# Two of seven Strassen sums started fresh at a change of groups and added by VectorE, with the first pairs' parts and the foldings moved in the written order

## Chip, cores, metric

One core of one Trainium2 chip runs the whole program in one launch. The time is device microseconds of one execution, as a median of three runs.

## What is computed

A hybrid decoder trunk of two layers over 256 positions of width 2048, all in float32: a short gated convolution and an MLP, then multi-head latent attention and an MLP, each followed by a layer norm of the residual. The change lies in the two MLPs:

```python
def sq_relu_mlp(x, w1, w2):          # w1: 2048 x 8192, w2: 8192 x 2048
    return jnp.square(jax.nn.relu(x @ w1)) @ w2

h = layer_norm(ALPHA * h + sq_relu_mlp(h, mlp_w1[layer], mlp_w2[layer]), ...)
```

## The kernel before

**Numbers.** A float32 factor is split into a high part, rounded by ScalarE (`hi`, L139), and the rest, subtracted by VectorE (`lo`, L140). TensorE multiplies high by high, high by low and low by high. Each weight tile of 128x1024 comes by DMA into one of seven `raw` tiles and costs one ScalarE cast and one VectorE subtraction.

**Passes and slots.** The 8192 hidden columns go in eight passes `q` of eight chunks `m` of 128 columns. In pass 0 everything is done plainly. From pass 1 on the up-projection of one chunk (a *unit*: 32 matmuls into the PSUM bank `unit`) is fused with down-projection work of an earlier chunk pair. One turn of the loop over (q, m) is a *slot*. The unit leaves its bank by `whole` (L399 on ScalarE into `t`, L400 on VectorE into `fp`), which is called the evacuation; the next unit needs the bank.

**Fast products.** For passes 1 to 6 (`FAST`; in the second MLP also half of pass 7) the down projection of a pair of chunks is done with seven products in place of eight, after Strassen and Winograd: four additions on the activations (`form`, L688 to L691; the results are split into the factors `h1a`, `h1c` and so on by `finish_pair`) and four on the weights (`prepare`, L172 to L179: `raw_t`, then the tiles `11`, `T1`, `21` and the others). Each of the seven products adds to a sum of its own in a PSUM bank. They are issued in the order of `FACTORS`: 3, 1, 5, 7, 2, 6, 4. Products of a pair lag the units by five slots.

**Groups.** The seven sums cover one group of 1024 of the 2048 output columns at a time. After four pairs of a pass the other group's turn comes: the change of groups, in the slot m = 0 of the next pass. All seven sums are then stored (`put_back`, L653) to their places in SBUF, and those of the other group are loaded into the same banks (`resume`, L738), both by ScalarE with 0.6 us copies. Sums 1, 5, 7 and 6 (`OWN`) have places of their own in `sums` and begin fresh the first time; 2, 3 and 4 have theirs in the accumulator `acc`. Four of the seven moves are spread over the slot of the change, and three lie in the next slot, which is called *crowded* in the code: there the evacuation comes ahead of the products.

**Folding.** At the end the eight additions of `fold` for each group combine the sums into `acc` (L661). The first MLP then goes on with pass 7 plainly (`down`); its residual, parked in DRAM meanwhile, comes back into the tile that `sums` had (L880, on POOL's queue; L452 is its first use). The second MLP ends with `down_late`, where the last additions (`fold_last`, L672) and the last layer norm are done on what is still in PSUM.

**Order.** Within the slots the order of the instructions of TensorE, VectorE and ScalarE is the written one: `Order.keep` ties each instruction to the one before it on its engine. Outside the slots, and on the queues of SP and POOL, a planner orders them by its own costs. `move(n)` does n of the waiting moves, `to_step(n)` brings the next slot's weight pair to its step n, `split_due` splits factors that are due, and `far` is a pair two slots ahead in the first slots of a MLP, which have no products yet.

## Time and profile before

| | |
|---|---|
| median of three runs | 2024.12 us (2024.03 to 2024.38) |
| the profiled execution | 2027.43 us, its span 2025.6 us |
| mean granted TensorE clock | 0.997 |
| busy: TensorE | 1993.8 us (98%) |
| busy: VectorE | 1754.5 us (87%) |
| busy: ScalarE | 1298.8 us (64%) |
| fused passes of the first MLP | about 452 to 1006 us of the span |
| fused passes of the second MLP | about 1408 to 1996 us of the span |

A row of a timeline gives start, duration, engine, line and operation; in brackets the idle time of the engine just before it and who ended it. A row `a <- b` of the waits gives who waited for whom: total, times and the longest. Matmuls are pipelined: one of 512 columns is shown with 0.39 us but they follow each other faster, so busy time of TensorE counts no work, while a gap in it is a gap. A row of the windows gives busy time by engine (TensorE, its weight loads, VectorE, ScalarE, POOL), then the granted clock, the DMA share and GB/s. PE is TensorE, DVE is VectorE, ACT is ScalarE.

### The profile page before, as it was taken

The page shows a single profiled execution, that of the slowest core. Times are in us where ns is not written, and L with a number is a line of the kernel's source. Part 1 is how long each engine was busy: PE and PEld are TensorE (multiplying, and loading weights), DVE is VectorE, ACT ScalarE, POOL GpSimd, SP SyncE. Part 2 cuts the span into 40 slices and gives each one's busy share as a digit, 9 for nine tenths or more (in the row PEclk, how much of TensorE's full clock was granted, in tenths as well). Part 3 has the DMA queues.
Part 4 walks back from the last instruction along what each step waited for, and adds up shares of the span by engine and source line. Part 5 has one row for each costly group of instructions (what it writes and reads, how often), then busy time and mean ns, then how long its engine had stood idle before and what let it go on. Part 6 is the DMA issues. An engine that isn't in the chain of part 4 may idle for free.

```text
span 2025.6 us, 29534 instructions
## 1 busy us (share of the span) xinstructions
PE 1993.8 (98%) x11050; PEld 1731.1 (85%) x11050; DVE 1754.5 (87%) x2539; ACT 1298.8 (64%) x1915; POOL 5.6 (0%) x27
## 2 busy tenths in 40 slices
PE   9999999999999999999999999999999999999998
PEld 8888888988888888888879998898888888888886
DVE  8667677777999999999989988777899999999998
ACT  7444445576767767677746665557667776767763
POOL 0000000000000000000000000000000000000000
PEclk9999999999999999999999999999999999999999
DMA  9766666574665566655765544565456656566554
GB/s 346 207 189 187 189 193 189 180 226 126 207 207 191 186 206 206 202 188 194 241 205 180 180 130 144 178 196 158 140 195 206 205 188 202 194 208 196 186 191 156
DMA packets 107710, 389.98 MB, mean 193 GB/s; under 512 B 11952, under 2 KB 12720, under 8 KB 107056
## 3 DMA queue, kind: packets, MB, share of 16 engines
q1 hardware_dynamic: 106560, 383.79, 59.1%
q0 software_dynamic: 864, 4.19, 0.6%
q8 instruction: 86, 1.41, 0.3%
q14 instruction: 56, 0.46, 0.1%
q10 hardware_dynamic: 144, 0.13, 0.0%
HBM read 383.87 MB, written 4.19 MB: 192 GB/s over the span
## 4 chain that ended last, share of the span: by engine, by line
PE 49%; DVE 37%; issue 7%; ACT 6%; DMA 0%; DVEq 0%; ACTq 0%
DVE lo L140 13%; PE ps_l L255 13%; PE ps_l L259 7%; DVE lo_t L140 5%; DVE raw_t L172 4%; PE ps_u L255 3%; DVE raw L179 3%; DVE raw L177 3%; DVE t L140 2%; PE ps_d L343 2%; PE ps_d L342 2%; PE ps_d L340 2%; ACT hi L139 2%; PE ps_w L289 2%; PE ps_w L288 2%
## 5 line engine op out<-in xcount | busy, mean ns | idle before, releaser
L140 DVE TENSOR_TENSOR lo<-raw,hi 128x1024 fp32r<-128x1024 f32 x710 | 853.4, 1221 | 138.9 <-ACT hi L139 69.7
L139 ACT CAST hi<-raw 128x1024 fp32r<-128x1024 f32 x710 | 729.2, 1049 | 353.7 <-DVE raw L177 141.8
L255 PE MATMUL ps_u<-xhl,hi 128*128 128x512 f32 x1792 | 624.3, 395 | 12.7 <-DVE fp L400 12.6
L259 PE MATMUL ps_u<-xhl,lo 128*128 128x256 f32 x1792 | 486.8, 281 | 0.0
L255 PEld LDWEIGHTS ps_u<-xhl,hi 128*128 128x128 f32 x1792 | 330.0, 188 | 84.7 <-DVE fp L400 18.4
L259 PEld LDWEIGHTS ps_u<-xhl,lo 128*128 128x128 f32 x1792 | 339.2, 189 | 12.3
L255 PE MATMUL ps_l<-xhl_a,hi 128*128 128x512 f32 x704 | 244.1, 393 | 0.0
L259 PE MATMUL ps_l<-xhl_a,lo 128*128 128x256 f32 x704 | 195.5, 280 | 0.0
L255 PEld LDWEIGHTS ps_l<-xhl_a,hi 128*128 128x128 f32 x704 | 132.2, 188 | 29.8
L259 PEld LDWEIGHTS ps_l<-xhl_a,lo 128*128 128x128 f32 x704 | 131.9, 188 | 0.2
L172 DVE TENSOR_TENSOR raw_t<-raw,raw 128x1024 f32<-128x1024 f32 x100 | 121.9, 1219 | 0.0
L140 DVE TENSOR_TENSOR lo_t<-raw_t,hi_t 128x1024 fp32r<-128x1024 f32 x100 | 121.9, 1219 | 0.0
L139 ACT CAST hi_t<-raw_t 128x1024 fp32r<-128x1024 f32 x100 | 105.2, 1052 | 3.9 <-DVE raw_t L172 3.9
L399 ACT COPY t<-ps_u 128x256 f32<-128x256 f32 x112 | 41.1, 367 | 89.5 <-PE ps_u L259 89.5
L255 PE MATMUL ps_l<-z,hi 128*128 128x512 f32 x240 | 82.4, 391 | 0.0
L400 DVE TENSOR_TENSOR fp<-ps_u,t 128x256 f32<-128x256 f32 x112 | 47.2, 421 | 35.3 <-ACT t L399 35.3
L289 PE MATMUL ps_w<-xd,hi 128*128 128x258 f32 x256 | 72.8, 284 | 0.0
L287 PE MATMUL ps_w<-xd,hi 128*128 128x258 f32 x256 | 72.3, 283 | 0.0
L288 PE MATMUL ps_w<-xd,lo 128*128 128x258 f32 x256 | 72.3, 283 | 0.0
L179 DVE TENSOR_TENSOR raw<-raw 128x512 f32<-128x512 f32 x100 | 69.2, 692 | 3.5
L140 DVE TENSOR_TENSOR t<-raw,t 128x512 fp32r<-128x512 f32 x100 | 68.6, 686 | 3.5 <-ACT t L139 3.5
L255 PE MATMUL ps_l<-oT,hi 128*128 128x512 f32 x208 | 71.3, 392 | 0.0
(361 smaller groups left out, 3908.2 us busy)
## 6 DMA issues: line engine op xcount, KB each, us to landing
raw<-in_w_dram SPq DMA_DIRECT2D x312, 512.0 KB, 4.2
raw<-in_w2f_dram SPq DMA_DIRECT2D x200, 512.0 KB, 4.1
raw<-in_w_in_dram SPq DMA_DIRECT2D x88, 512.0 KB, 4.3
raw<-in_w_out_dram SPq DMA_DIRECT2D x32, 512.0 KB, 4.3
raw<-in_w_o_dram SPq DMA_DIRECT2D x32, 512.0 KB, 4.1
raw<-in_w_kv_dram SPq DMA_DIRECT2D x10, 512.0 KB, 4.8
raw<-in_w_q_dram SPq DMA_DIRECT2D x8, 512.0 KB, 4.1
raw<-in_w_uk_dram SPq DMA_DIRECT2D x8, 512.0 KB, 4.4
```

The lines of the kernel that those rows point to most:

```text
L139: nc.scalar.copy(hi, src)
L140: return nc.vector.tensor_tensor(lo, src, hi.bitcast(F32), ALU.subtract)
L172: nc.vector.tensor_tensor(t.rearrange(two, a=2), b12.unsqueeze(1).to_broadcast([P, 2, BW]), r1.rearrange(two, a=2), ALU.subtract)
L177: nc.vector.tensor_tensor(b12, b22, t[:, :BW], ALU.subtract)
L179: nc.vector.tensor_tensor(t4, b21, b12, ALU.subtract)
L255: nc.tensor.matmul(ps, w[blk // 8][0][:, blk % 8, :], x, start=first, stop=False)
L259: nc.tensor.matmul(ps[:, :T], w[blk // 8][1][:, blk % 8, :], x[:, :T], start=False, stop=last)
L287: nc.tensor.matmul(ps[:, :W], hi, x[k][:, :W], start=k == 0, stop=False)
L288: nc.tensor.matmul(ps[:, :W], lo, x[k][:, :W], start=False, stop=False)
L289: nc.tensor.matmul(ps[:, :W], hi, x[k][:, W:], start=False, stop=k == NC - 1)
L399: nc.scalar.copy(t, ps[:, T:])
L400: nc.vector.tensor_tensor(out, ps[:, :T], t, ALU.add)
```

## The change

1. Sums 6 and 4 (`ADDED`) are no longer loaded at a change of groups: their first matmul starts the bank anew, and when they are stored, VectorE adds the bank to the place in SBUF (`tensor_tensor`) where ScalarE copied before. Sum 6 begins fresh the first time in each group as before. At the last change of the second MLP (`keep`) both are loaded again by ScalarE, because that MLP's end works on the whole sums in PSUM.
2. In the slot of a change (m = 0) the factors of the last pair (`split_due`) are split ahead of the two single weight tiles, not behind the first of them.
3. `prepare` of a pair has one step more: the two 512-column subtractions are a step of their own. The pair two slots ahead (`far`) does two steps ahead of the evacuation and two behind it, where it did three behind.
4. The order of the eight additions in `fold` is another, and they are done elsewhere: in the first MLP all of the first group at the end of slot m = 4 of pass 7, the second group's in slots 6 and 7 ahead of the evacuation (before: five in each of slots 5, 6 and 7 behind it, one after the loop); in the second MLP three in slot 7 of pass 7, two among the last slot's single tiles, three after the loop (before: one in each of slots 1 to 7 and one after).
5. In pass 7 of the first MLP the last pair's factors are split in two halves, each in its turn. In the second MLP one last sum is loaded (`last_sum`) at the start of the last slot, not after the loop, and the last pair's factors are split in slot 7.

```diff
@@ prepare
         nc.vector.tensor_tensor(t4, b21, b12, ALU.subtract)
+        yield
         finished(t, f"{i}_t")
@@ size
-        return 1 if len(stream[i]) == 1 else 5
+        return 1 if len(stream[i]) == 1 else 6
@@
     OWN = ("1", "5", "7", "6")
+    ADDED = ("6", "4")
@@ put_back, fold
-            nc.scalar.copy(place(p, g), ps)
+            if p in added:
+                nc.vector.tensor_tensor(place(p, g), place(p, g), ps, ALU.add)
+            else:
+                nc.scalar.copy(place(p, g), ps)
...
-            for d, a, b in ((c[1][0], c[1][0], s1), (s6, s6, s1), (c[1][1], c[1][1], s6), (s7, s7, s6),
-                            (c[0][0], c[0][0], s7), (c[0][1], c[0][1], s7), (c[1][1], c[1][1], s5), (c[0][1], c[0][1], s5)):
+            for d, a, b in ((s6, s6, s1), (s7, s7, s6), (c[0][0], c[0][0], s7), (c[0][1], c[0][1], s7),
+                            (c[0][1], c[0][1], s5), (c[1][0], c[1][0], s1), (c[1][1], c[1][1], s6), (c[1][1], c[1][1], s5)):
@@ resume, move
-        def resume(p, g, at=None):
-            ps[p] = psum(f"ps_{p}", bank[at or p])
+        def resume(p, g, keep=False):
+            ps[p] = psum(f"ps_{p}", bank[p])
             onto.discard(p)
+            added.discard(p)
             if p in OWN and opened[g] == FAST[0]:
                 fresh.add(p)
+            elif p in ADDED and not keep:
+                fresh.add(p)
+                added.add(p)
             else:
                 nc.scalar.copy(ps[p], place(p, g))
                 onto.add(p)
...
-                        resume(o, 1 - g)
+                        resume(o, 1 - g, last and on == FAST[-1])
@@ new
+        def columns(m):
+            if q in FAST or last:
+                return (slice(P if q in FAST else 0, 8 * P),) if m % 2 else ()
+            if m >= QC - 2:
+                return (slice(m % 2 * T, (m % 2 + 1) * T),)
+            return (slice(0, 2 * T),) if m % 2 else ()
+
+        def fold_some(n):
+            for _ in range(n):
+                next(folds, None)
@@ the slot
             crowded = len(moves) > 0
+            ends = q == NQ - 1 and m == QC - 1
+            if q == NQ and last:
+                last_sum(0, 0, bank["unit"])
             to_step(1)
-            if not singles:
+            if not singles or m == 0 or q == NQ:
                 split_due()
-            for i in singles:
+            for n, i in enumerate(singles):
+                if q == NQ and n == 4:
+                    fold_some(2)
                 step(i)
                 move(1)
                 split_due()
             if crowded:
                 evacuate()
                 move(len(moves))
+            if far:
+                for i in far:
+                    for _ in range(2):
+                        step(i)
+            if q == NQ - 1:
+                fold_some((3 if ends else 0) if last else 5 if m == QC - 2 else 3 if ends else 0)
...
             move(1)
             to_step(3)
-            move(1)
+            if ends:
+                split_due()
             to_step(4)
             move(1)
             to_step(5)
+            move(1)
+            to_step(6)
             move(1)
...
-                if q == NQ - 1:
-                    for _ in range((m > 0) if last else 5 if m >= SHIFT else 0):
-                        next(folds, None)
+                if q == NQ - 1 and m == SHIFT - 1 and not last:
+                    fold_some(8)
                 for i in far:
-                    for _ in range(3):
+                    for _ in range(2):
                         step(i)
```

More of the change, by code (lines that the diff above doesn't have):

```diff
@@ L696, in forms, with finish_pair @@
                 form(u)
-        def finish_pair(j, u, of):
+        def finish_pair(j, u, at):
             f = factors[j // 2][:, j % 2]
-            at = slice(P, 8 * P) if of in FAST else slice(0, 8 * P) if last else slice(0, 2 * T)
             split(f[:, 0, at], f[:, 1, at], u[:, at])
@@ L727, in mlp @@
         factors = [act.tile([P, QC // 4, 2, 8 * P], F32R, tag=tag, name=f"h{idx}{tag}") for tag in ("c", "a2")]
-        ps, onto, fresh = {}, set(), set()
+        ps, onto, fresh, added = {}, set(), set(), set()
         folds = iter(())
-        def resume(p, g, at=None):
-            ps[p] = psum(f"ps_{p}", bank[at or p])
+        def resume(p, g, keep=False):
+            ps[p] = psum(f"ps_{p}", bank[p])
             onto.discard(p)
+            added.discard(p)
             if p in OWN and opened[g] == FAST[0]:
                 fresh.add(p)
+            elif p in ADDED and not keep:
+                fresh.add(p)
+                added.add(p)
             else:
@@ L763, in products_of @@
                 opened[g] = 0
-                moves.extend((o, g, i == 0 and p < NQ - 1) for o in order if p < NQ - 1 or o in OWN)
+                moves.extend((o, g, p if i == 0 and p < NQ - 1 else 0) for o in order if p < NQ - 1 or o in OWN)
                 if p == FAST[-1]:
@@ L777, in split_due @@
             while due:
-                j, of = due.pop()
-                finish_pair(j, rows.pop(j), of)
+                j, at = due.pop()
+                finish_pair(j, rows[j], at)
+        def columns(m):
[7 more added lines that the diff above has]
+                next(folds, None)
         for s, (q, m, pair, own) in enumerate(slots):
@@ L817, in evacuate @@
                     forms(u)
-                    due.append((m // 2, q))
+                    due.extend((m // 2, at) for at in columns(m))
             crowded = len(moves) > 0
+            ends = q == NQ - 1 and m == QC - 1
+            if q == NQ and last:
+                last_sum(0, 0, bank["unit"])
             to_step(1)
-            if not singles:
+            if not singles or m == 0 or q == NQ:
                 split_due()
-            for i in singles:
+            for n, i in enumerate(singles):
+                if q == NQ and n == 4:
+                    fold_some(2)
                 step(i)
@@ L836, in mlp @@
                 if hi_first:
-                    for i in pairs:
-                        step(i)
+                    to_step(2)
                 evacuate()
@@ L854, in mlp @@
                         forms(u)
-                        due.append((m // 2, q))
+                    due.extend((m // 2, at) for at in columns(m))
                 if extra and q == FAST[0] and m < NB:
@@ L873, in mlp @@
         if last:
-            for n, t, o in ((0, 0, "unit"), (1, 0, "1"), (0, 1, "5"), (1, 1, "7")):
+            for n, t, o in ((1, 0, "1"), (0, 1, "5"), (1, 1, "7")):
                 last_sum(n, t, bank[o])
```

## The prediction

> **What bounds the kernel now.** I read the page first, then the list of waits, then the timeline of each engine around the longest waits.

> ```profile
> PE 1993.8 (98%) x11050; PEld 1731.1 (85%) x11050; DVE 1754.5 (87%) x2539; ACT 1298.8 (64%) x1915; POOL 5.6 (0%) x27
> PE 49%; DVE 37%; issue 7%; ACT 6%; DMA 0%; DVEq 0%; ACTq 0%
> ```

> TensorE is busy for 98% of the span, so little more than its idle time can be won. But 37% of the chain that ended last lies on VectorE: there are places where VectorE, not TensorE, sets the pace. The list of waits names two of them in the fused passes, and TensorE's timeline shows where they lie.

> ```profile
> PE ps_u L255 <- DVE fp L400: 12.6, 12, 1.9
> PE ps L343 <- DVE h1a L140: 2.6, 6, 1.4
> ```

> ```profile
> 519.71 0.51 PE L343 MATMUL ps<-hi,h1a 128*128 128x512 f32 x1 [1.42 <-DVE h1a L140]
> ...
> 603.17 0.50 PE L343 MATMUL ps<-hi,h1a 128*128 128x512 f32 x1 [0.21 <-DVE h1a L140]
> ...
> 607.62 0.39 PE L255 MATMUL ps_u<-xhl,hi 128*128 128x512 f32 x1
> ...
> 617.98 0.39 PE L255 MATMUL ps_u<-xhl,hi 128*128 128x512 f32 x1
> ...
> 629.69 0.50 PE L255 MATMUL ps_u<-xhl,hi 128*128 128x512 f32 x1 [1.18 <-DVE fp L400]
> ...
> 714.61 0.50 PE L255 MATMUL ps_u<-xhl,hi 128*128 128x512 f32 x1 [1.19 <-DVE fp L400]
> ...
> 1930.12 0.56 PE L255 MATMUL ps_u<-xhl,hi 128*128 128x512 f32 x1 [1.92 <-DVE fp L400]
> ```

> Read these as follows. A slot is one up-projection unit and one pair's products. Two slots follow each other without a wait at 607.62 and 617.98: 10.36 us. A pass of eight slots should take 82.9 us, but the stall at 629.69 comes back at 714.61, 84.92 us later. So each change of groups costs 2.04 us: 629.69 should have been 628.34, which is 1.35 of it (the unit waits until VectorE has emptied the one `unit` bank, L400), and the other 0.69 falls where TensorE waits for the low part of pair 3's factors (603.17, L140). The same two waits stand at four changes of each MLP. The first change of each has a larger one (519.71) and a sixth only the small one. All TensorE can regain in the passes is about 2 us for each of twelve changes.

> Why is VectorE late there? Its own rows in the slot after a change, and ScalarE's beside them:

> ```profile
> 610.28 1.22 DVE L172 TENSOR_TENSOR raw_t<-raw,raw 128x1024 f32<-128x1024 f32 x1
> 611.76 1.23 DVE L140 TENSOR_TENSOR lo<-raw,hi 128x1024 fp32r<-128x1024 f32 x1 [0.26 <-ACT hi L139]
> 613.84 1.23 DVE L140 TENSOR_TENSOR lo<-raw,hi 128x1024 fp32r<-128x1024 f32 x1 [0.85 <-ACT hi L139]
> 615.25 0.42 DVE L400 TENSOR_TENSOR fp<-ps_u,t 128x256 f32<-128x256 f32 x1 [0.18 <-ACT t L399]
> 617.34 1.23 DVE L140 TENSOR_TENSOR lo<-raw,hi 128x1024 fp32r<-128x1024 f32 x1 [1.67 <-ACT hi L139]
> ```

> ```profile
> 612.76 1.05 ACT L139 CAST hi<-raw 128x1024 fp32r<-128x1024 f32 x1
> 613.71 0.58 ACT L653 COPY sums<-ps 128x512 f32<-128x512 f32 x1
> 614.32 0.59 ACT L738 COPY ps<-sums 128x512 f32<-128x512 f32 x1
> 614.85 0.37 ACT L399 COPY t<-ps_u 128x256 f32<-128x256 f32 x1
> 615.11 0.59 ACT L653 COPY acc<-ps 128x512 f32<-128x512 f32 x1
> 615.74 0.59 ACT L738 COPY ps<-acc 128x512 f32<-128x512 f32 x1
> 616.26 1.05 ACT L139 CAST hi<-raw 128x1024 fp32r<-128x1024 f32 x1
> ```

> VectorE waits four times, 2.96 us in all, each time for ScalarE, which works without a gap: between its casts it stores a sum (L653) and reloads the next (L738), 0.6 us each. The last `lo`, at 617.34, waits 1.67 us for a cast that is queued behind sums 6 and 4. From there VectorE has no gap until TensorE stalls at 629.69. The chain is: TensorE's first product, ScalarE's copies, VectorE, TensorE.

> **The change, part by part.** *Sums 6 and 4 by VectorE.* In the slot above, ScalarE loses the four copies from 613.71 to 615.74: `t` comes at 613.71, the cast behind it ends at 615.1 in place of 617.31. VectorE gains two additions of a PSUM bank to 128x512 numbers (sum 4 at every change, sum 6 from the third: 12 in the first MLP, which also stores its last group so, 10 in the second). The nearest row is the same form:

> ```profile
> L661 DVE TENSOR_TENSOR acc<-acc,sums x18: 681/690/696, 995.3 to 1986.6; 128x512 f32<-128x512 f32 x18
> L643 DVE TENSOR_TENSOR acc<-acc,ps_d x8: 686/692/693, 1016.6 to 1057.6; 128x512 f32<-128x512 f32 x8
> ```

> ```profile
> 600.90 1.22 DVE L140 TENSOR_TENSOR lo<-raw,hi 128x1024 fp32r<-128x1024 f32 x1
> 602.03 1.09 DVE L140 TENSOR_TENSOR h1a<-fp,h1a 128x896 fp32r<-128x896 f32 x1
> ```

> L643 takes 0.692 us with a PSUM operand, L661 0.690 us without. [...] The two rows here differ by 2 ns, so I go by them.

> One VectorE instruction starts 0.09 us before the one ahead of it ends (600.90 + 1.22 against 602.03). Laid end to end from the `lo` at 613.84, which stays where ScalarE puts it: addition of 6 at 614.97, `fp` at 615.58, addition of 4 at 615.91, `lo` at 616.52. That is 0.82 us earlier than 617.34, although VectorE does 1.2 us more. What follows on VectorE comes 0.82 us earlier too, so the stall at 629.69 shrinks from 1.35 to 0.53 us. Sum 4's bank is free at 616.6; its product starts at about 617.3, so nothing new waits, by 0.7 us. If the additions took 0.3 us longer each, that cover would be gone.

> *Pair 3's parts ahead of the singles.* At 602.03 the factors' low part moves ahead of the `lo` at 600.90, 1.13 us earlier; it was late by 0.69. That wait goes; the `lo` that moves back is needed only 5 us later. Together a middle change costs about 0.6 us in place of 2.04. I take 1.4 us for each of eight: 11.2; the sixth change gives 0.6 in each MLP: 1.2.

> *The first pair of each MLP.* Two of its preparing steps go ahead of the evacuation in the slot before it:

> ```profile
> 474.91 0.42 DVE L400 TENSOR_TENSOR fp<-ps_u,t 128x256 f32<-128x256 f32 x1 [3.37 <-ACT t L399]
> ...
> 477.70 1.22 DVE L172 TENSOR_TENSOR raw_t<-raw,raw 128x1024 f32<-128x1024 f32 x1
> ```

> ```profile
> 446.52 3.04 SPq L150 DMA_DIRECT2D raw<-in_w2f_dram  x2
> ```

> VectorE is idle there for 3.37 us; the subtraction of 477.70 and the `lo` behind it (2.3 us) fit in. Their two loads on SP's queue, which move with them, were issued at 446.52, so no data are waited for. With the 1.13 us of pair 3's parts this covers the 1.7 us lost at 519.71 (1.42 idle and a slow restart) and part of two small waits ahead of it: 2.5 us in each MLP, 5.0. The extra yield in the pair's preparation changes no order elsewhere.

> *The last change of the second MLP* keeps sums 6 and 4 in PSUM. ScalarE's reload of 6 must now wait for VectorE's addition, and the evacuation and the cast stand behind that reload; the same again for 4. Laid end to end, the last `lo` of that slot comes 2.0 us later than before: minus 2.0. The stall at 1930.12 stays.

> *Folds of the first MLP.*

> ```profile
> 995.00 0.42 DVE L400 TENSOR_TENSOR fp<-ps_u,t 128x256 f32<-128x256 f32 x1 [3.45 <-ACT t L399]
> ...
> 1013.72 0.70 DVE L661 TENSOR_TENSOR acc<-acc,sums 128x512 f32<-128x512 f32 x1
> ...
> 1021.80 0.29 DVE L452 TENSOR_SCALAR xback<-xback 128x256 f32<-128x256 f32 x1 [3.91 <-DMA xback<-parked]
> ```

> ```profile
> 1014.72 1.63 POOL L880 DMA_DIRECT2D xback<-parked  x3 [0.25 <-DVE acc L661]
> ```

> ```profile
> 1000.00:1025.00 25.00, 21.24 (x96) 17.43 (x96) 20.80 (x33) 12.45 (x18) 2.69 (x5) 0.95 0.80 255
> ```

> All 16 folds stand behind 995.00 now; eight of them (0.6 us each, 4.8) move into the 3.45 us of idle ahead of it. The last ends at 1014.4, and only then may the parked residual be loaded into the same tile: issue at 1014.72, data at 1021.80. TensorE waits for it (21.24 busy of 25: 3.76 us lost) and then runs at a granted clock of 0.95 in this window, 1.25 us more. After the change the last three folds stand ahead of the last `fp`, and with VectorE's instructions laid end to end the last one ends, as an estimate, 5.0 us after the last unit's last matmul in place of 8.4: two `lo`, 0.4 us of the last pair's parts and three folds stand behind the evacuation before it, where now two evacuations, eight folds and four `lo` do. The wait falls to about 0.4 us, the slow clock goes with it: 3.4 + 1.25, of which I take 4.1. Two bounds: 1.1, if POOL's load stays behind its memset of `kpe`, which waits for the last factors; 5.0, if both go fully.

> *Folds of the second MLP* move from one in each slot of the last pass to its end.

> ```profile
> 1985.68 0.49 PE L340 MATMUL ps_e<-hi,h3c 128*128 128x512 f32 x1 [1.79 <-ACT hi L139]
> ...
> 1988.47 0.79 PE L342 MATMUL ps_e<-lo,h3c 128*128 128x512 f32 x1 [1.11 <-DVE lo L140]
> ```

> ```profile
> 1994.76 0.70 DVE L672 TENSOR_TENSOR ps<-ps,sums 128x512 f32<-128x512 f32 x1 [0.66 <-PE ps L343]
> 1996.40 0.69 DVE L672 TENSOR_TENSOR sums<-sums 128x512 f32<-128x512 f32 x1 [0.94 <-ACT sums L653]
> ```

> The pass gets lighter and the waits at 1985.68 and 1988.47 nearly go, but the six folds must be done later. From 1917 to the end VectorE has only two gaps, 0.66 and 0.94 us. So the end is VectorE's: it gains what that engine gained earlier, and at most these 1.6 us; I take 0.8.

> **Sum.** 11.2 + 1.2 + 5.0 - 2.0 + 4.1 + 0.8 = 20.3 us from the profiled 2027.43 us (span 2025.6, 1.8 around it): 2007.1. The three timed runs have a median of 2024.12, 3.3 lower, so 2003.8.

> **The rivals.** *The ends give nothing back.* POOL's order keeps the first MLP's wait and VectorE's 1.6 us stay: 11.2 + 1.2 + 5.0 - 2.0 + 1.1 - 1.1 = 15.4 at most, 14.3 without the 1.1: 2009.8. For: all folds are still done, and nothing outside the slots has its order written. Against: the row at 1014.72 waits for a fold, not for the memset. The granted clock is priced in this: a stall of 2.3 us ahead of 1930.12 already led to 0.57 in the next 4 us.

> ```profile
> 1930.00:1934.00 4.00, 3.88 (x13) 3.33 (x14) 3.97 (x6) 3.30 (x4) 0.00 (x0) 0.57 0.43 122
> ```

> [...]

> *TensorE sets the last end.* If VectorE's work at the end can be spread under TensorE's, the second MLP also wins the two late waits with their slow restart, 6 us more than taken: 1997.8. Against: VectorE has no gap there.

> *VectorE becomes the bound: slower.* The additions lie on the engine that is late. If its waits after a change are not ScalarE's copies, or its `lo` waits on in their place, 22 additions of 0.61 us come on top: 13.4 us, 2037.5. It decides in the slot after a change: as soon as the `lo` starts later than 617.34 seen from the change, every change loses. For: VectorE's four waits of 2.96 us above are nearly all its slack in 84.92 us. Against: the row at 617.34 names ScalarE, and ScalarE loses 2.3 us just ahead of it.

> *It does less than it says.* Waits shift from the one place to the other within a pass and the time stays within 0.2%, which is what a measurement of this kernel can tell from none: 2022.

> **How the numbers follow.** Forecast 0.60; ends give nothing 0.20; TensorE sets the end 0.10; slower 0.07; no difference 0.03. Predicted 2003.8. From 1996 to 2012 the range takes in the first three cases and the bounds of the additions and of the residual's load; 0.10 is left out, besides errors of size. Faster 0.90, same 0.03, slower 0.07.

> **What the changed profile would show.** Right: the stalls at a unit's start return every 83.5 us and are under 0.8; no wait for pair 3's factors at the middle changes; the last `lo` after a change waits for nothing; additions of 0.69 us from PSUM; a stall of 2 us or more remains in the second MLP's last pass; the gap at the residual is under 1 us. Wrong: passes still 84.9 us or longer, a `lo` after a change that waits for ScalarE over 1 us, a product 4 that waits for VectorE in the middle passes, or a new gap between 1985 and the end.

## The result, and the profile after

After runs in 2010.37 us (median of four: 2009.04 to 2011.72), before beside it in 2024.25 us: a ratio of 0.9929, with an interval from 0.9912 to 0.9947. That is 13.9 us less. The forecast was 2003.8 us with a range from 1996 to 2012. The profiled execution took 2011.46 us with a span of 2009.6 us, against a span of 2025.6 us before: 16.0 us less, where the working had 20.3.

From the page of after (busy times; shares of the chain) and from its waits:

```profile
PE 1990.4 (99%) x11050; PEld 1730.7 (86%) x11050; DVE 1764.9 (88%) x2562; ACT 1275.1 (63%) x1872; POOL 5.6 (0%) x27
PE 82%; DVE 10%; ACT 5%; issue 3%; DMA 1%; DVEq 0%; ACTq 0%
```

```profile
PE ps L1225 <- ACT umeans L1222: 4.8, 1, 4.8
PE ps_u L256 <- DVE fp L402: 4.1, 7, 2.1
PE mu0p L456 <- DVE xback L454: 2.8, 1, 2.8
```

VectorE's share of the chain fell from 37% to 10%: in the passes TensorE now sets the pace. TensorE's wait for the evacuation fell from 12.6 us to 4.1, and its wait for the low part of pair 3's factors is gone from the list of the first MLP (2.6 us before); in the second one of 0.6 us is left, in the last pass. Two waits outside the passes now stand beside it. TensorE's timeline of after shows where (line numbers have moved by a few: L256 is the unit, L402 the evacuation, L657 stores or adds a sum, L747 loads one, L667 is a fold):

```profile
708.63 0.50 PE L256 MATMUL ps_u<-xhl,hi 128*128 128x512 f32 x1 [0.35 <-DVE fp L402]
...
792.17 0.50 PE L256 MATMUL ps_u<-xhl,hi 128*128 128x512 f32 x1 [0.34 <-DVE fp L402]
...
1900.30 0.50 PE L341 MATMUL ps<-t,h3c 128*128 128x512 f32 x1 [0.86 <-ACT ps L747]
...
1913.73 0.50 PE L256 MATMUL ps_u<-xhl,hi 128*128 128x512 f32 x1 [2.06 <-DVE fp L402]
```

The stall at a unit's start now returns after 83.54 us and is 0.35 us. At the last change of the second MLP the first product waits 0.86 us for a reload (1900.30), and the unit behind it still waits 2.06 us. VectorE in the slot behind a change:

```profile
693.62 1.23 DVE L140 TENSOR_TENSOR lo<-raw,hi 128x1024 fp32r<-128x1024 f32 x1 [0.85 <-ACT hi L139]
694.76 0.68 DVE L657 TENSOR_TENSOR sums<-sums,ps 128x512 f32<-128x512 f32 x1
695.36 0.42 DVE L402 TENSOR_TENSOR fp<-ps_u,t 128x256 f32<-128x256 f32 x1
695.69 0.68 DVE L657 TENSOR_TENSOR acc<-acc,ps 128x512 f32<-128x512 f32 x1
696.29 1.22 DVE L140 TENSOR_TENSOR lo<-raw,hi 128x1024 fp32r<-128x1024 f32 x1
```

It goes as it was laid end to end: addition, `fp`, addition, and a last `lo` that waits for nothing.

Units are the common marks of both traces, so the gain can be read from where each one starts (TensorE's timeline, first matmul of the unit):

| the same unit | before | after | difference |
|---|---|---|---|
| first fused unit of the first MLP | 452.10 | 452.19 | +0.09 |
| eight units on, past the first pair | 565.67 | 562.92 | -2.75 |
| past the four middle changes | 926.04 | 917.37 | -8.67 |
| past the sixth change, last slots | 988.83 | 979.57 | -9.26 |
| first fused unit of the second MLP | 1408.18 | 1400.13 | -8.05 |
| past its first pair | 1525.63 | 1514.43 | -11.20 |
| past its four middle changes | 1865.37 | 1848.12 | -17.25 |
| past the sixth change | 1907.31 | 1889.59 | -17.72 |
| past the last change | 1930.12 | 1913.73 | -16.39 |
| end of the span | 2025.6 | 2009.6 | -16.0 |

The passes won more than was forecast; both ends gave something back.

### The profile page after: what moved, and what is told of

Its sections match the earlier page's. It is cut to its first block, busy times and chain, and to the rows that moved or that the text cites. A ratio compares the mean times of both kernels' runs of the same rounds, so it can differ in the third digit from the quotient of the medians.

```text
span 2009.6 us, 29519 instructions
## 1 busy us (share of the span) xinstructions
PE 1990.4 (99%) x11050; PEld 1730.7 (86%) x11050; DVE 1764.9 (88%) x2562; ACT 1275.1 (63%) x1872; POOL 5.6 (0%) x27
## 3 DMA queue, kind: packets, MB, share of 16 engines
q8 instruction: 86, 1.41, 0.3%
## 4 chain that ended last, share of the span: by engine, by line
PE 82%; DVE 10%; ACT 5%; issue 3%; DMA 1%; DVEq 0%; ACTq 0%
PE ps_u L256 16%; PE ps_l L256 13%; PE ps_u L260 8%; PE ps_l L260 7%; PE ps L343 6%; PE ps L344 6%; PE ps L341 5%; DVE lo L140 4%; PE ps_d L344 2%; PE ps_d L343 2%; PE ps_d L341 2%; ACT hi L139 2%; PE ps_w L290 1%; PE ps_w L288 1%; PE ps_w L289 1%
## 5 line engine op out<-in xcount | busy, mean ns | idle before, releaser
L140 DVE TENSOR_TENSOR lo<-raw,hi 128x1024 fp32r<-128x1024 f32 x710 | 851.2, 1219 | 122.4 <-ACT hi L139 53.6
L139 ACT CAST hi<-raw 128x1024 fp32r<-128x1024 f32 x710 | 727.4, 1049 | 351.7 <-DVE raw L177 144.5
L256 PE MATMUL ps_u<-xhl,hi 128*128 128x512 f32 x1792 | 622.2, 394 | 4.1 <-DVE fp L402 4.1
L256 PEld LDWEIGHTS ps_u<-xhl,hi 128*128 128x128 f32 x1792 | 329.1, 187 | 73.9 <-DVE fp L402 7.4
L260 PEld LDWEIGHTS ps_u<-xhl,lo 128*128 128x128 f32 x1792 | 338.1, 189 | 12.6
L256 PE MATMUL ps_l<-xhl_a,hi 128*128 128x512 f32 x704 | 244.1, 393 | 0.0
L256 PEld LDWEIGHTS ps_l<-xhl_a,hi 128*128 128x128 f32 x704 | 132.1, 188 | 29.9
L140 DVE TENSOR_TENSOR lo_t<-raw_t,hi_t 128x1024 fp32r<-128x1024 f32 x100 | 121.8, 1218 | 0.0
L172 DVE TENSOR_TENSOR raw_t<-raw,raw 128x1024 f32<-128x1024 f32 x100 | 121.8, 1218 | 0.0
L139 ACT CAST hi_t<-raw_t 128x1024 fp32r<-128x1024 f32 x100 | 105.2, 1052 | 0.0
L256 PE MATMUL ps_l<-z,hi 128*128 128x512 f32 x240 | 82.4, 391 | 0.0
L256 PE MATMUL ps_l<-oT,hi 128*128 128x512 f32 x208 | 71.3, 391 | 0.0
L887 ACT ACTIVATE fp<-fp 128x512 f32<-128x512 f32 (+1 forms) x112 | 64.6, 577 | 7.6 <-DVE fp L402 5.8
L402 DVE TENSOR_TENSOR fp<-ps_u,t 128x256 f32<-128x256 f32 x112 | 46.7, 417 | 25.8 <-ACT t L401 25.6
```

Source lines behind the costliest of these rows:

```text
L139: nc.scalar.copy(hi, src)
L140: return nc.vector.tensor_tensor(lo, src, hi.bitcast(F32), ALU.subtract)
L172: nc.vector.tensor_tensor(t.rearrange(two, a=2), b12.unsqueeze(1).to_broadcast([P, 2, BW]), r1.rearrange(two, a=2), ALU.subtract)
L256: nc.tensor.matmul(ps, w[blk // 8][0][:, blk % 8, :], x, start=first, stop=False)
L260: nc.tensor.matmul(ps[:, :T], w[blk // 8][1][:, blk % 8, :], x[:, :T], start=False, stop=last)
```

## The experiments

Each kernel is after with one edit; the last three join several. Since a median moves by 1 to 2 us from run to run, the verdicts rest on the starts of units against after, and the medians stand beside them.

**Undoing one part: the additions.** Edit: `ADDED = ()`.

> After, but ScalarE stores and reloads all seven sums again (no sum is added by VectorE). Theory A, the additions take ScalarE's copies out of VectorE's way: from the after profile each of the middle changes won 0.84 us at the unit behind the crowded slot (the unit starts 0.84 us earlier against before, on top of 0.5 us from pair 3's parts). So the passes go from 83.55 to about 84.4 us, the stalls at a unit's start from 0.34 to about 1.2 us, at four changes of each MLP: 6.7 us; the last change of the second MLP gets 1.3 us back, since no reload stands behind VectorE. Span about 2015.0 against 2009.6, median about 2015.5. Theory B, the additions cost VectorE what they win and the gain is that of the other moves: passes stay at 83.5 us, span 2008 to 2010.

Measured: 2015.57 us, ratio to before 0.9953 (0.994 to 0.9967), span 2013.3. The passes of the first MLP lose 4.1 us (0.48 to 4.59), 1.35 at the first change and 0.8 to 0.9 at each of three others; those of the second lose 4.0 (2.71 to 6.72), and the last change gives 1.9 back (6.72 to 4.84). The wait that the additions take away is back, VectorE first and TensorE behind it:

```profile
699.12 1.22 DVE L140 TENSOR_TENSOR lo<-raw,hi 128x1024 fp32r<-128x1024 f32 x1 [1.66 <-ACT hi L139]
```

```profile
711.47 0.50 PE L256 MATMUL ps_u<-xhl,hi 128*128 128x512 f32 x1 [1.19 <-DVE fp L402]
```

Theory A holds, and the price of the reload behind VectorE, 2.0 in the prediction, is 1.9.

**Undoing one part: pair 3's parts.**

```diff
-            if not singles or m == 0 or q == NQ:
+            if not singles or q == NQ:
```

> After, but the last pair's factors at a change are split behind the first single weight tile again, as before. Theory A, the parts ahead of the singles win 0.5 us at each change on their own: TensorE's wait for the low part of pair 3's factors comes back, 0.2 us idle and a slow restart, 0.5 us at each of ten changes and about 1 us at each MLP's first pair; passes 84.1 us, span about 2016, median about 2016.5. Theory B, with ScalarE's copies gone VectorE is early enough in any order: no wait for the low part, passes 83.5 us, span 2009.6 within 0.5.

Measured: 2014.95 us, ratio 0.9949 (0.9937 to 0.9962). The first MLP loses 2.7 us in its passes, 0.7 at the first pair and 0.5 at each of four later changes; the second 3.05, 1.05 and four times 0.5. The row of the wait is back:

```profile
683.96 0.50 PE L344 MATMUL ps<-hi,h1a 128*128 128x512 f32 x1 [0.28 <-DVE h1a L140]
```

Theory A; only the first change of each MLP doesn't need it. The span, 2013.1 us, is less than the expected 2016, mostly since the first MLP's end is 2.3 us shorter here than in after.

**Undoing one part: the far pair's early steps.**

```diff
-            if far:
-                for i in far:
-                    for _ in range(2):
-                        step(i)
...
-                    for _ in range(2):
+                    for _ in range(4):
```

> After, but the pair two slots ahead does all its four steps behind the evacuation, none ahead of it. Theory A: the first pair of each MLP won 2.75 and 3.15 us against before, of which pair 3's parts are about 1 us each; the rest comes back: 3.5 to 4.5 us, all of it between the second and the fifth fused unit of each MLP; span 2013 to 2014, median about 2014.5. Theory B, all of it was pair 3's parts: the first five units of each MLP start as in after, span 2009.6 within 0.5.

Measured: 2014.58 us, ratio 0.9942 (0.993 to 0.9955). The first MLP loses 1.83 us up to its ninth unit, the second 2.18, and nothing after that. With the 0.7 and 1.05 us of pair 3's parts that makes 5.8 of the 6.0 us that the first pairs won. The first MLP's end is 2.6 us shorter here, so the span, 2012.1 us, is only 2.5 us longer than that of after.

Undone one at a time, the three parts give back 15.9 of the 17.7 us that the passes won, the last change included. No run here says to which part the other 1.8 us belong.

**Undoing one part: the places of the folds.** All additions of `fold` back to the end of slots 5, 6 and 7 and after the loop, in the second MLP one in each slot; their new order among themselves stays.

> After, but the additions of fold at their old places in both MLPs. Theory of the prediction: their move wins 4.1 us at the first MLP's end and 0.8 at the second's, so this kernel is 4.9 us slower than after: span 2014.5. Theory A, from the after profile: the move won nothing, since TensorE waits 2.76 us for the residual (3.76 before) but then runs 6.83 us at half clock (3.41 before), and at the very end it waits 4.79 us (1.58 before) and runs its last matmuls at half clock. By that this kernel has the wait of 3.8 us for the residual again, with one stretch of 3.41 us at half clock, and its last matmuls at full clock: the first end within 1 us of after, the second 1 to 2.4 us shorter; span 2007 to 2009.6.

Measured: 2010.03 us (2009.19 to 2010.89), ratio 0.9924 (0.991 to 0.9937): no slower than after. At the first MLP's end it is 1.94 us *faster* than after (0.20 to -1.74). POOL's load of the residual and the first matmul on it, in after and then in this kernel:

```profile
1003.74 1.64 POOL L914 DMA_DIRECT2D xback<-parked  x3 [564.16 <-DVE fp L402]
...
1011.61 1.22 PE L456 MATMUL mu0p<-xback,ones 128*128 128x256 f32 x2 [2.76 <-DVE xback L454]
```

```profile
1008.97 1.64 POOL L910 DMA_DIRECT2D xback<-parked  x3 [5.53 <-DVE acc L667]
...
1015.79 0.70 PE L456 MATMUL mu0p<-xback,ones 128*128 128x256 f32 x2 [3.07 <-DVE xback L454]
```

The load is issued 5.2 us earlier in after and its data are there 4.2 us earlier, and TensorE waits only 0.3 us less. Between the last unit and that matmul, TensorE's timeline has 71 products here and 47 in after, where five more stand between the units. So TensorE is out of products 3.9 us earlier in after (1008.85 against 1012.72): outside the slots the planner orders, and it drew the matmul forward by nearly as much as the data came earlier. In the second MLP the old places cost 1.9 us in the last pass, of which the end gives 0.9 back: there the move is worth 1.0 us.

**Two ways to take the residual's wait away.** First, the load still earlier: `8 if m == QC - 2 else 0` in place of `5 if m == QC - 2 else 3 if ends else 0`, so that all folds of the second group stand ahead of slot 6's evacuation.

> After, but all eight additions of the first MLP's second group stand ahead of the evacuation of slot 6 of the last pass, none in slot 7. Theory A, the residual's load is issued when the last fold is done (1003.21 us, issue at 1003.74) and lands 7.5 us later: the last fold now ends some 6 us earlier, the load is issued near 997.5 us and lands near 1005, ahead of TensorE's last product at 1008.85 us. TensorE's wait of 2.76 us falls under 0.5, and the 6.83 us at half clock behind it (3.1 us lost) go with it: the second MLP's first unit starts 5 to 6 us earlier, span 2003.5 to 2005. Rival B, the load waits for the last evacuation, which the trace names as its releaser (VectorE, fp): issue stays near 1003.7 us and the end stays within 1 us of after. Rival C, the wait goes but the clock falls all the same for other small gaps: 2.8 us, span about 2007.

Then the matmul later, the load left alone:

```diff
             down(h, put, n)
-            prepare_chunks(range(4 * n, 4 * n + 4))
             if n:
+                prepare_chunks(range(4 * n - 4, 4 * n))
                 turned(n - 1)
+        prepare_chunks(range(4 * NB - 4, 4 * NB))
```

> After, but the preparation of each four chunks of the residual is written behind the next block of down, so that in the order of TensorE's instructions 91 products stand between the first MLP's last unit and the first matmul on the residual, where after has 46, before 56 and the kernel with the old folds 71. Theory A: the early folds did bring the load forward (issue 1003.74 us, old folds 1008.97), but the planner brought the first matmul forward by as much (25 products of 0.227 us, 5.7 us), so the wait stayed at 2.8 to 3.1 us. With 45 products more ahead (10.2 us) TensorE finds the residual there: no wait at the first MLP's end and no stretch at half clock, 2.8 us and 1.7 or 3.1 us: span 2004 to 2005.5. Rival, the residual's chain is the bound whatever stands ahead of it: the wait appears later, ahead of the attention, and the span is 2009.6 within 1.

Measured: 2004.88 us, ratio 0.99 (0.9886 to 0.9913), and 2005.56 us, ratio 0.9899 (0.9882 to 0.9915). The load and the matmul with the early folds, and the matmul with 91 products ahead of it; neither matmul waits:

```profile
998.10 1.64 POOL L914 DMA_DIRECT2D xback<-parked  x3 [558.10 <-DVE fp L402]
...
1010.06 0.59 PE L456 MATMUL mu0p<-xback,ones 128*128 128x256 f32 x2
```

```profile
1018.49 0.59 PE L456 MATMUL mu0p<-xback,ones 128*128 128x256 f32 x2
```

Each wins 5.7 to 6.1 us at that place (second unit of the second MLP 5.75 and 5.68 us earlier than in after), twice the wait. The spans, 2002.8 and 2003.7 us, are a little below what was expected. The other half is the clock. The windows of after, 3.41 us each (busy times by engine; the third figure from the end is the granted clock):

```profile
1007.58:1010.99 3.41, 1.27 (x6) 0.72 (x4) 0.03 (x1) 1.04 (x1) 0.00 (x0) 1.00 0.97 320
1010.99:1014.40 3.41, 2.79 (x7) 2.24 (x8) 3.14 (x6) 0.37 (x1) 1.07 (x2) 0.50 1.01 405
1014.40:1017.81 3.41, 3.41 (x10) 2.67 (x9) 3.41 (x6) 1.05 (x1) 0.00 (x0) 0.50 1.01 385
```

Behind the wait TensorE runs 6.83 us at half clock: its matmuls of 512 columns start every 0.43 us there (1013.05 to 1017.32) and every 0.23 us behind it (1018.48 to 1019.17). From 1011.61 on that costs an estimated 2.9 us of work by these two figures (3.1 in the expectations, half of the stretch); in before, with one such window and the same two figures, 1.6 us.

**The clock at the very end.** Four float32 matmuls into a PSUM bank that nobody reads, where TensorE has nothing to do while VectorE finishes the last layer norm's first half:

```diff
...
+            busy = psum("busy", state["free"])
+            for i in order:
+                nc.tensor.matmul(busy, id_t, state["us"][i], start=True, stop=True)
```

> After, with four added matmuls of 128x512 float32 numbers into a PSUM bank that nobody reads, between TensorE's last product (1994.6 us) and the first matmul of the last layer norm's second half (1999.38 us); their operands are ready by 1995.3 us. Clock theory: the 4.79 us in which TensorE waits there are why its clock is halved from 1997.44 to 2004.26 us, and the matmuls behind it (3.78 us in a row of the after profile, 1.98 us for the two in the before profile) take 2.4 us more than they would. With the added matmuls, some 0.98 us each by the before profile, the clock stays full: span 2007.2, median about 2008.0. Rival, the end is set by VectorE's chain alone, or the added matmuls stand in the way: span 2009.6 within 0.3, or up to 1 us longer.

Measured: 2007.17 us, ratio 0.9908 (0.9894 to 0.9921), span 2005.9. TensorE's end, first in after, then with the added matmuls (each of them has two records):

```profile
1999.38 3.78 PE L1225 MATMUL ps<-gbt,umeans 128*128 128x512 f32 x4 [4.79 <-ACT umeans L1222]
```

```profile
1993.26 3.60 PE L1225 MATMUL busy<-u,id_t 128*128 128x512 f32 x8
1998.04 1.98 PE L1230 MATMUL ps<-gbt,umeans 128*128 128x512 f32 x4 [1.18 <-ACT umeans L1227]
```

The same matmuls take 1.98 us here, as in before, and 3.78 in after, where the granted clock is 0.50 from 1997.44 to 2004.26 us. From the first of them to the end of the span it is 7.8 us here, 7.9 in before and 10.3 in after: 2.4 us, as the clock theory had it. The units of the second MLP already start 1.2 us earlier than in after, since this run has one window at half clock at the first MLP's end in place of two; that is nearly all of the other 1.3 us.

**The last change of the second MLP.** `elif p in ADDED and not (keep and p == "4")`: only sum 4 is loaded again.

> After, but at the last change of the second MLP only sum 4 is loaded again; sum 6 begins fresh and is added to its place by VectorE at the end. The kernel without additions got 1.9 us back at that change. Theory A, the two reloads that stand behind VectorE's additions cost about half of it each: the units behind the last change start 0.9 us earlier than in after, VectorE does one addition of 0.6 us more at the end, which it sets: span 2009.2 to 2009.6. Rival, the reload of 4 alone holds the slot: units start as in after or later, span 2009.6 to 2010.5.

Measured: 2008.87 us, ratio 0.9917 (0.9904 to 0.9931). The slot behind the last change starts 1.05 us earlier (-1.41 to -2.46), so each of the two reloads costs half; VectorE's addition more at the end doesn't show. The span of 2007.0 us lies below both expectations because 1.4 us were won ahead of that change already, at the first MLP's end, with one window at half clock there. What remains is the other one, waiting for VectorE's addition:

```profile
1897.20 0.59 ACT L747 COPY ps<-acc 128x512 f32<-128x512 f32 x1 [2.55 <-DVE acc L657]
```

**A third sum.** `ADDED = ("2", "6", "4")`.

> After, with a third sum, 2, begun fresh and added by VectorE. Rival of the prediction, VectorE becomes the bound: in the slot behind a change it waits only 1.1 us in all in the after profile (0.25 ahead of 691.54 and 0.85 ahead of 693.62), so a third addition of 0.6 us at each change comes on top: the stall at a unit's start grows from 0.34 to about 0.9 us, passes 84.1 us, and the last change of the second MLP loses up to 0.9 us more by a third reload: span 2014 to 2016. Theory A, what VectorE waits for are ScalarE's two copies of that sum (691.42 and 692.02 us): the addition fits into the 0.85 us, the cast behind the copies comes 1.1 us earlier, and the stall of 0.34 us goes: passes 83.2 us, 0.3 us less at each of eight changes, 0 to 0.9 us more at the last change: span 2007 to 2008.5, if the same stretches are at half clock.

Measured: 2007.7 us, ratio 0.9909 (0.9894 to 0.9924). Passes of 83.2 us; 1.1 us won in the first MLP's and 1.0 in the second's, 1.4 lost at the last change. The addition fills the hole in front of the second `lo`:

```profile
692.36 0.68 DVE L657 TENSOR_TENSOR acc<-acc,ps 128x512 f32<-128x512 f32 x1
692.96 1.22 DVE L140 TENSOR_TENSOR lo<-raw,hi 128x1024 fp32r<-128x1024 f32 x1
```

So VectorE wasn't the bound even with 35 additions in place of 22. The span, 2004.4 us, is lower than either theory had it, since the clock stays full at the first MLP's end in this run: 3.5 us (1.1 us earlier than after at its last units, 4.6 behind it).

**Versions that beat both.** Early folds and added matmuls together; with sum 6 not loaded again; and with a third sum in the first MLP alone (`ADDED[last:]`).

> After, with both the added matmuls at the end and the first MLP's folds ahead of slot 6's evacuation. Theory A with the clock theory: both gains add, 5 to 6 us at the first MLP's end and 2.4 us at the last: span 2001 to 2003, median about 2003, faster than before by 1.1%. If the load's issue stays or the added matmuls bring nothing, it is the better of the two alone.

> After, with the early folds of the first MLP, the added matmuls at the end and only sum 4 loaded again at the last change. The kernel with the first two ran 2002.9 us; the third alone won about 1 us at the last change's first slot. Theory A, they add: median 2001.5 to 2002.5. Rival, at the end VectorE's one addition more takes back what the change won: 2002.9 within 0.5.

> The kernel with the early folds, the added matmuls and sum 6 not loaded again (2002.2 us), and besides a third sum, 2, added by VectorE in the first MLP alone, where no last change reloads it. By the kernel with three sums, the units of the first MLP's last pass start 1.38 us earlier than in after. Theory A, the gains add: span about 1999.0, median about 2000.8. Rival, the first MLP's end, which is set by the residual's load and VectorE's folds, takes it back: 2002.2 within 0.5.

Measured: 2002.9 us, ratio 0.989 (0.9876 to 0.9903); 2002.22, ratio 0.9882 (0.9868 to 0.9897); 2001.37, ratio 0.9882 (0.9865 to 0.9898). The gains add by the starts of units: sum 6 not loaded again wins 1.06 us at the last change in the second of these kernels, where the medians are only 0.7 apart. Of the 1.38 us expected of the last step 0.25 were an earlier start of the run with three sums; the passes won 1.0 and the median 0.85.

## Why the prediction was right or wrong

| step of the prediction | forecast, us won | measured |
|---|---|---|
| eight middle changes | 11.2 | 12.0 (5.9 + 6.05) |
| sixth change | 1.2 | 1.1 |
| first pairs | 5.0 | 6.0 (2.84 + 3.15) |
| last change of the second MLP | -2.0 | -1.3 |
| first MLP's end | 4.1 | -1.2 |
| second MLP's end | 0.8 | -0.4 |

With the 0.09 us by which after began later, these make the 16.0.

**The slots were right, by their own reasons.** VectorE waited for ScalarE's copies (without the additions the 1.66 us wait is back), the additions win 0.8 to 0.9 us a change as laid end to end, pair 3's parts 0.5. The sign of a reload behind VectorE's addition was right, and its price: 1.9 where it is undone, 2.0 forecast. The rival in which VectorE becomes the bound is excluded by passes of 83.2 us with three sums.

**The step that failed is "the wait falls to about 0.4 us, the slow clock goes with it".** The wait in before, and the last fold of after:

```profile
1022.14 0.93 PE L454 MATMUL mu0p<-xback,ones 128*128 128x256 f32 x2 [3.76 <-DVE xback L452]
```

```profile
1002.52 0.69 DVE L667 TENSOR_TENSOR acc<-acc,sums 128x512 f32<-128x512 f32 x1
```

The fold ends 5.2 us after the last unit, 5.0 were forecast; in before it was 8.8 by the rows, where the prediction has 8.4. The load's issue, 0.5 us behind it, and the data, 7.5 us behind that, took 0.7 us longer than in before; why is not shown. Together the residual comes 2.9 us earlier behind the last unit, 0.5 less than the 3.4 taken. The matmul was taken to stay where it stood behind that unit; with 47 products between them in place of 56, TensorE runs out of products 11.0 us behind the unit in place of 12.9, 1.9 us sooner. So 2.76 us of wait were left, 2.4 more than forecast, where the prediction named a gap under 1 us as a sign of being right. The last unit was no fixed mark either: five of the products now stand ahead of it, and it ends 1.6 us later, counted from the unit at 979.57 us (988.83 in before). From there the last fold is only 2.0 us earlier than in before, and the data 1.3. The half clock, which was to go, lasted two windows in place of one. With one window, as in the kernels without the additions, with the added matmuls and with sum 6 fresh, this end is 1.8 to 1.9 us shorter, but so it is with the folds at their old places: moving them as after does was worth nothing at this end; moved further, with the early folds, they won 6.1 us there.

**The second end was right for VectorE and missed TensorE.** VectorE's aggregate of the last layer norm, in before and in after:

```profile
2016.96 0.26 DVE L1167 BATCH_NORM_AGGREGATE mv<-stats 128x2 f32<-128x24 f32 x1
```

```profile
1998.57 0.26 DVE L1201 BATCH_NORM_AGGREGATE mv<-stats 128x2 f32<-128x24 f32 x1
```

It comes 18.4 us earlier, 2.0 more than the unit past the last change, where 0.8 was taken; up to there the end is VectorE's, and its two gaps did go. But TensorE, which now finishes its products sooner, idles 4.79 us instead of 1.58 ahead of its last matmuls and does them at half clock: minus 2.4. The prediction named a new gap in this stretch as a sign against it, and priced none. A half-clock window behind the last change costs nothing there: with the added matmuls TensorE's units fall back by 1.5 us after it, and VectorE's aggregate doesn't.

The likeliest case asked both ends to pay. What happened is nearest to the first rival, that the ends give nothing: 2009.8 against 2010.37 measured, for a reason it only half had (not POOL's order, but the planner's and the clock). That the figures lie so near is partly luck: the ends lost 1.6 us, and the passes won 17.7 where 15.4 were taken. The forecast too was helped by this, since the two ends came out 6.5 us short and the passes hid 2.3 of it. Of the 6.6 us between 2003.8 and the median, 4.3 are these terms; most of the rest is the conversion, since the profiled before lay 3.3 us above its median and the profiled after 1.1.

The prediction's price for the clock took a stall of 2.3 us ahead of 1930.12; by the row it shows, TensorE stood still for 1.92 us there.

**The additions from PSUM.** The 22 additions with a PSUM operand against the folds, which have none:

```profile
L667 DVE TENSOR_TENSOR acc<-acc,sums 128x512 f32<-128x512 f32 x18 | 11.9, 686 | 0.2
L657 DVE TENSOR_TENSOR acc<-acc,ps 128x512 f32<-128x512 f32 x13 | 8.8, 677 | 0.0
L657 DVE TENSOR_TENSOR sums<-sums,ps 128x512 f32<-128x512 f32 x9 | 6.1, 680 | 0.0
```

They are 6 to 9 ns shorter, so the rows of before, 2 ns apart, were a fair measure of what the additions would take.

## What to carry to other kernels

An engine that is 87% busy can still be the right place for more work, if what it waits for is the engine that the work is taken from: look at who ended its waits in the one slot that is late. When a load is brought forward, ask who places its first reader; where a planner does, it may spend the gain at once. And ahead of a wait of TensorE, price the clock behind it, or give TensorE something harmless to do: in before, a wait of 1.92 us inside one window of 3.41 us was followed by a window at a granted clock of 0.50.

## What was not expected of the hardware

| kernel | first MLP's end | at the last change | the end |
|---|---|---|---|
| before | 1 | 1 | 1 |
| after | 2 | 0 | 2 |
| old folds | 1 | 0 | 1 |
| added matmuls | 1 | 1 | 0 |
| early folds | 0 | 1 | 1 |
| three sums | 0 | 1 | 1 |
| early folds, added matmuls, sum 6 fresh | 0 | 0 | 0 |

The same stall of 2.06 us behind the last change leaves the clock full in after, where the grid cuts it into 0.43 and 1.62 us of idle time, and halves it with the added matmuls, where it lies in one window. After first, then the other:

```profile
1908.70:1912.11 3.41, 2.98 (x14) 2.13 (x12) 3.41 (x4) 3.24 (x5) 0.00 (x0) 1.00 0.80 262
1912.11:1915.52 3.41, 1.79 (x10) 1.56 (x11) 3.38 (x6) 1.21 (x2) 0.00 (x0) 1.00 0.69 233
1915.52:1918.94 3.42, 3.42 (x21) 3.02 (x20) 3.42 (x5) 3.21 (x4) 0.00 (x0) 1.00 0.17 38
```

```profile
1909.32:1912.73 3.41, 1.35 (x7) 0.81 (x6) 3.41 (x5) 1.50 (x3) 0.00 (x0) 1.00 0.58 197
1912.73:1916.14 3.41, 3.41 (x11) 2.93 (x12) 3.38 (x5) 2.96 (x4) 0.00 (x0) 0.50 0.32 120
```

At these three places of all the profiles a window with 1.76 us of TensorE's idle time or less (that with three sums, from 1008.44) kept the full clock, and one with 1.92 or more (that of before, from 1927.02) was followed by a window at half clock. Between them it went either way: 1.81 us with three sums lost it, 1.82 with the old folds kept it. A window at half clock with 0.62 us of idle time or more (after, from 1010.99) was followed by another, with 0.42 or less (without the additions, from 2003.50) by the full clock. These bounds hold for the windows seen here and were not tried one by one. Each such window that TensorE works through costs it an estimated 1.6 us, nearly half its length, by the 0.43 us from one matmul of 512 columns to the next where after is at half clock and the 0.23 us behind it.

That the runs of after fall into two pairs, 2009.0 to 2009.3 and 2011.5 to 2011.7 us, fits one window more or less at the places that TensorE sets, and the mean granted clocks of 0.997 and 0.996 agree with it. This is argued, not shown: only one of the four has a profile here, and it is one of the longer two, so the tables above are of such an execution.
